# Second-layer weight sums from a load of their own, a sixth pair of split weights, and two output tiles weighted by VectorE

## The chip, the cores and the metric

The kernel runs on one core of one Trainium2 chip, as one launch. The metric is the time of an execution in device microseconds (us); lower is better. TensorE does the matrix products (the profile calls it PE, and its weight loads PEld), VectorE (DVE) and ScalarE (ACT) the work between them, GpSimd (POOL) issues the DMAs that add while they write and a few elementwise products, and SyncE (SP) issues the plain loads and stores. DMAs move data between HBM and the on-chip buffers.

## What is computed

One layer of a decoder trunk on 512 tokens of width 1024, in float32: a norm, one projection whose columns feed three groups of heads (dilated windows, gated linear attention, block-sparse attention), an output projection, a second norm, a feed-forward block of width 4096, and a final norm. The part that matters here is the end:

```python
x = x + mix @ w_out
h2 = rmsnorm(x, norm2_w)
x = x + jnp.square(jax.nn.relu(h2 @ w_ff1)) @ w_ff2
...
y = xf * lax.rsqrt(jnp.mean(xf * xf, axis=-1, keepdims=True) + EPS)
return (y * w.astype(jnp.float32)).astype(x.dtype)
```

## The kernel before

**Products in two halves.** Matrix products run on a reduced 32-bit type. Each operand is split into a high part `wh` (or `Ah`, `xh`, `yp`) that ScalarE makes by a copy, and a low part `wl` (`Al`) that VectorE makes by a subtraction; a product is then three matmuls: high by high, low by high, high by low. `parts` (line 282) splits a weight tile of 128 x 1024.

**The feed-forward block.** It has four chunks c of 1024 hidden columns, and each chunk two units: (1, c) makes `h` from the normed input and `w_ff1`, and (2, c) multiplies the squared `h` by `w_ff2` and adds to the residual `x3`. Each unit is a two-by-two block product done with seven products instead of eight (the Strassen-Winograd scheme). They run in the order of `PRODUCTS` (line 32), by number 0, 1, 3, 5, 2, 4, 6; the letters X, Y and Z name the accumulators, so the trace shows `f1X`, `f1Y`, `f1Z`, `f2X` and so on. Product 0 uses weight quadrant (0,0), product 1 uses (1,0), and the rest use sums of quadrants (with the signs put into the stored weights and the other operand). Every product comes in two halves, `ip` 0 and 1, with a weight tile of 512 KB each.

**Weight sums.** `fetch_ff` (line 316) loads the quadrants by SP in the order of `loads` (line 395). `sums_ff` (line 335) turns them into the sums: `plus` is a POOL DMA that adds a quadrant from HBM into a tile that is already there, `add` a VectorE addition. The main chain of a unit is one tile that becomes the operand of products 3, 2 and 6 in turn, by adding (0,1), then (1,1), then (1,0), each time only after the operand before has been split (`done(n)`: the event that `cut_ff`, line 406, fires). In the second-layer units that tile is the one of product 0 itself, so (0,1) is added only after product 0's split.

**The order of work.** `Plan` (class at line 101) writes the order of each engine's queue when the program is built. Streams of work (Python generators) are run against a clock with a cost for each operation; at each step it issues the operation that can start first, and by priority where several can. Costs are in `Op`: a DMA's size is divided by a rate, 280e3 bytes per us for a plain one and 170e3 for an adding one (line 78). `("wait", key)` and `("take", resource)` hold back a stream in the plan alone; on the chip, an operation starts when it is at the head of its engine's queue and the data and buffers that it touches are free. Tokens bound how far work runs ahead: `w` is the number of pairs of split weights (5, line 29: `WPAIRS`; the out-projection hands them back one by one in `let_go`, line 1072, and the last unit gets 3 more), `raw2` the raw weight tiles, `big` all large buffers (`BIGS`, 24, of 4 KB a partition). `SLOTS` (54, of 2 KB a partition) is the number of small buffers, which the plan doesn't model.

**The end.** `add` (line 1187) adds each product's accumulator to `x3`. When a half of a token tile t (0 to 3) is complete, `square_sum` (line 933) sums its squares. The half of a tile that is complete first is multiplied by the final norm's weights on POOL (`weighted`, line 1204, tile `xw`; `fw` is the weights); when the other half is complete, `final` (line 1211) makes the inverse root, weights and scales that other half on VectorE (tile `of`), scales `xw` on ScalarE, and stores both. For tiles 0 and 1 the first half is complete after product 1 of the last unit, for tiles 2 and 3 after product 4.

Of the kernel before, what the change touches and what calls it, by code (L numbers as in the profile page):

```python
# [13 lines left out]
OP = mybir.AluOpType  # L14
# [11 lines left out]
KO = (3, 4, 0, 1, 2, 5, 6, 7)  # L26
TAU = 1.0 / 16.0
LC, LT, LW, LN, WARM = 1.0, 0.5, 1.0, 0.0, 9
BIGS, SLOTS, WPAIRS = 24, 54, 5
NC = 4  # L30
LAG = 3
PRODUCTS = ((0, "X", True, ((0, 0),)), (1, "Y", True, ((0, 0),)), (3, "Z", True, ((1, 1),)), (5, "Z", False, ((0, 1),)),
# [3 lines left out]
class Op:  # L36


    def __init__(self, eng, method, args, kw):
        self.eng, self.method, self.args, self.kw = eng, method, args, kw  # L40
        self.out = args[0]
        outs = [args[0]]
        inner = [a for a in list(args[1:]) + [v for k, v in kw.items() if k != "accum_out"] if isinstance(a, bass.AP)]
        if kw.get("accum_out") is not None:
            outs.append(kw["accum_out"])
        if method == "tensor_tensor_reduce":
            outs.append(inner.pop())
        self.outs = [o.tensor.name for o in outs]
        self.ins = [a.tensor.name for a in inner] + (self.outs if "accum_op" in kw else [])
        n = 1  # L50
        for c in args[0].shape[1:]:
            n *= c
        if eng == "tensor":
            wide, long = inner[-1].dtype == F32, max(n, 250) / 2400
            if method != "matmul":
                self.cost = 0.109
            elif wide and inner[-1].shape[0] == 32:
                self.cost = 0.031
            elif wide:
                self.cost = 0.002 + max(n / 600 / (1 + (args[0].shape[0] == 64)), 0.21)  # L60
            elif inner[-1].shape[0] == 64:
                self.cost = max(n / 2260, 0.12) / 2
            else:
                self.cost = 0.0135 + long
        elif eng == "scalar":
            few = sum(a.shape[-1] == 1 and n > 4 for a in inner) + ("accum_out" in kw)
            self.cost = 0.09 + n / 1200 + 0.093 * few
        elif eng == "vector":
            many = method in ("tensor_scalar", "tensor_copy") and all(a.space == bass.MemoryType.SB for a in inner)
            rate = 0.52 if many else 6.25 if method == "reciprocal" else 1.04  # L70
            if method == "tensor_reduce":
                n = 512
            self.cost = 0.075 + n * rate / 1000
        elif eng == "gpsimd":
            self.cost = 0.15 + n * (0.9 if method == "memset" else 2.1) / 1000
        if method == "dma_start":
            self.cost = 0.9 if "accum_op" in kw else 0.06
            self.rate = 170e3 if "accum_op" in kw else 280e3
            self.size = 4 * n * args[0].shape[0]


# [16 lines left out]
PE, ACT, DVE, POOL, SP = (Engine(n) for n in ("tensor", "scalar", "vector", "gpsimd", "sync"))  # L98


class Plan:
# [17 lines left out]
    def fire(self, key, t=None):  # L119
        self.done[key] = self.now if t is None else t  # L120
# [78 lines left out]
def hybrid_block_kernel(ctx: ExitStack, tc: tile.TileContext, xT_d, x_d, w0_d, wv_d, wqk_d, wo_d, w1_d, w2_d,  # L199
# [9 lines left out]
    plan = Plan(nc, dict(BANKS, raw=3, w=WPAIRS, big=BIGS, raw2=3, part=5, lev=4, cnt=1))  # L209
    spawn, fire, give = plan.spawn, plan.fire, plan.give  # L210
    late = dict(copy=LC, tt=LT)

    def slot(name, dt=F32, shape=(128, 512)):
        return sp.tile(list(shape), dt, name=name, tag="slot", bufs=SLOTS)
# [4 lines left out]
    def small(name, shape):  # L219
        return sp.tile(list(shape), F32, name=name, tag="small_" + "_".join(map(str, shape)), bufs=16 if shape[1] <= 2 else 3)  # L220
# [110 lines left out]
    def give_raw():  # L331
        give("big")
        give("raw2")

    def sums_ff(u, ip):


        def plus(t, q):
            yield POOL.dma_start(t, quad_d(u, q, ip), accum_op=OP.add)

        def add(a, b):
            yield DVE.tensor_tensor(a, a, b, op=OP.add)

        def made(n, t):
            B[u, n, ip] = t
            fire(("B", u, n, ip))

        def done(n):
            yield ("wait", ("cut", u, n, ip))

        def loaded_(n):
            yield ("wait", ("quad", u, n, ip))
            return quads[u, n, ip]

        t = yield from loaded_(0)
        made(0, t)
        made(1, (yield from loaded_(1)))
        if u == units[0]:
            give_after(u, 0, ip)
            t = yield from loaded_(3)  # L360
            yield from plus(t, (0, 1))
            made(3, t)
            made(5, (yield from loaded_(5)))
            give_after(u, 5, ip)
            b12 = yield from loaded_(4)
            yield from plus(b12, (1, 1))
            made(4, b12)
            yield from done(3)
            yield from plus(t, (1, 1))
            made(2, t)  # L370
        else:
            b12 = None
            if u[0] == 1:
                b12 = yield from loaded_(4)
            b22 = yield from loaded_(5)
            made(5, b22)
            yield from done(0)
            yield from (add(t, b12) if b12 else plus(t, (0, 1)))
            made(3, t)
            yield from done(3)  # L380
            yield from plus(t, (1, 1))
            made(2, t)
            if b12:
                yield from add(b12, b22)
                made(4, b12)
                give_after(u, 5, ip)
            else:
                yield from done(5)
                yield from plus(b22, (0, 1))
                made(4, b22)  # L390
        yield from done(2)
        yield from plus(t, (1, 0))
        made(6, t)

    loads = {0: ((0, (0, 0)), (1, (1, 0)), (3, (0, 0)), (5, (1, 1)), (4, (0, 1))),
             1: ((0, (0, 0)), (1, (1, 0)), (4, (0, 1)), (5, (1, 1))),
             2: ((0, (0, 0)), (1, (1, 0)), (5, (1, 1)))}

    def give_after(u, n, ip):
        def stream():  # L400
            yield ("wait", ("cut", u, n, ip))
            give_raw()

        spawn(stream(), 0)
# [100 lines left out]
    st = {}  # L505
# [420 lines left out]
    x3 = {}  # L926
# [4 lines left out]
    ssq = {}  # L931

    def square_sum(t, half):

        q = small("ssq", (128, 1))
        yield ACT.activation(slot("junk"), x3[t, half], AF.Square, accum_out=q)
        if t in ssq:
            yield DVE.scalar_tensor_tensor(ssq[t], q, 1.0 / D, ssq[t], op0=OP.mult, op1=OP.add)
            fire(("ssq", t))
        else:  # L940
            ssq[t] = small("m", (128, 1))
            yield DVE.tensor_scalar(ssq[t], q, 1.0 / D, EPS, op0=OP.mult, op1=OP.add)

    def inv_rms(t):
        yield ("wait", ("ssq", t))
# [84 lines left out]
    def out_proj():  # L1030
# [41 lines left out]
        def let_go(i):  # L1072
            give("big")
            give("big")
            give("raw2")
            if i < WPAIRS:
                give("w")

        yield from take(2)
# [107 lines left out]
    def add(c, i, q, acc):  # L1187
        n, b_, _, targets = PRODUCTS[i]
        for blk, half in targets:
            t = 2 * blk + q  # L1190
            if c == NC - 1 and n != 6:
                yield ("prio", 1.3 + i)
            yield DVE.tensor_tensor(x3[t, half], x3[t, half], acc, op=OP.subtract if half and b_ == "X" else OP.add)
            if c == NC - 1 and not any((blk, half) in p[3] for p in PRODUCTS[i + 1:]):
                spawn(square_sum(t, half), -1 if n == 6 else 0)
                if t in ssq:
                    spawn(final(t, half), -1 if n == 6 else 0)
                else:
                    spawn(weighted(t, half), 9)
        if not any(p[1] == b_ for p in PRODUCTS[i + 1:]):  # L1200
            give(TAGS[2][b_][q])
        fire(("read", (2, c), b_, q))

    def weighted(t, half):
        yield ("wait", "fw")
        yield ("wait", ("w", ((2, NC - 1), 6, 1)))
        st["xw", t] = xw = slot("xw")
        yield POOL.tensor_tensor(xw, x3[t, half], fw[:, half * 512:half * 512 + 512], op=OP.mult)
        fire(("xw", t))

    def final(t, half):
        yield from inv_rms(t)
        y = st.pop(("inv", t))
        yield ("wait", ("xw", t))
        ts = slice(t * 128, (t + 1) * 128)
        a, b = (slice(h * 512, h * 512 + 512) for h in (half, 1 - half))
        of, xw = slot("of"), st.pop(("xw", t))
        yield DVE.scalar_tensor_tensor(of, x3[t, half], y, fw[:, a], op0=OP.mult, op1=OP.mult)
        yield SP.dma_start(out_d[ts, a], of)
        yield ACT.activation(xw, xw, AF.Copy, scale=y)  # L1220
        yield SP.dma_start(out_d[ts, b], xw)

    fw = None
# [202 lines left out]
```

## Time and profile before

| what | us |
|---|---|
| time, median of three runs | 590.65 (589.93 to 591.92) |
| the profiled execution's own time | 590.61 |
| its span, from the first to the last instruction | 588.8 |

The stages of that execution, with the busy time of the engines and the mean busy share of the DMA engines:

| stage | from to, us | PE | DVE | ACT | DMA share |
|---|---|---|---|---|---|
| first projection and gates | 0 to 34.8 | 31.5 | 23.3 | 22.1 | 0.84 |
| projections, attention, linear attention | 34.8 to 199.4 | 164.2 | 123.0 | 92.4 | 0.32 |
| output projection, second norm | 199.4 to 255.1 | 54.9 | 28.4 | 27.1 | 0.38 |
| unit (1, 0) | 255.1 to 298.0 | 41.9 | 36.5 | 34.7 | 0.74 |
| unit (2, 0) | 298.0 to 338.7 | 39.3 | 35.2 | 20.3 | 0.80 |
| units (1, 1) and (2, 1) | 338.7 to 417.2 | 78.4 | 66.1 | 49.6 | 0.74 |
| units (1, 2) and (2, 2) | 417.2 to 495.6 | 78.4 | 63.1 | 48.2 | 0.75 |
| unit (1, 3) | 495.6 to 535.9 | 40.3 | 27.0 | 26.7 | 0.62 |
| unit (2, 3) | 535.9 to 580.9 | 40.4 | 37.0 | 22.9 | 0.49 |
| after the last matmul | 580.9 to 588.8 | 0 | 2.6 | 2.5 | 0.35 |

A row such as `L129 DVE TENSOR_TENSOR h<-h,s x8: 684/687/3745` gives an engine, an operation, the tile written and the tiles read, the count, and the shortest, median and longest duration in ns. All operations are issued by one line (129) of the planner, so they are told apart by their tiles. `wraw` is a raw weight tile, `in_w` the weights in HBM. In an engine's queue in order of time, a row gives start, duration, operation, shapes and count; brackets give the idle time before it and what ended that. A share of a stretch in which the DMA engines are busy can read slightly over 1.

### The profile page before, as it was taken

How to read it: one execution, taken by the hardware profiler on the slowest of the kernel's cores; microseconds unless marked ns; L12 is line 12 of the kernel's file. 1: busy time of each engine (PE TensorE's matmuls, PEld its weight loads, DVE VectorE, ACT ScalarE, POOL GpSimd, SP SyncE). 2: the span in 40 equal slices, each digit the busy share in tenths (PEclk: the TensorE clock that was granted, in tenths of full speed). 3: DMA queues.
4: the chain of work that ended last, by engine and by line, in shares of the span. 5: the costliest groups of instructions: out<-in, count | busy, mean ns of one | idle time of the engine just before them, and what ended most of it. 6: DMA issues, size and time to landing. Idle time of an engine off the chain costs nothing.

```text
span 588.8 us, 9325 instructions
## 1 busy us (share of the span) xinstructions
PE 569.3 (97%) x3549; PEld 486.5 (83%) x3549; DVE 442.3 (75%) x788; ACT 346.4 (59%) x604; POOL 60.9 (10%) x81
## 2 busy tenths in 40 slices
PE   8999999999999999999999999999999999999794
PEld 7968888768876677899988699988999888998583
DVE  5789976754796724679789785799865998766994
ACT  6653426746585743667765356846377654676553
POOL 4020000000000000020012011120111110111301
PEclk9999999999999999999999999999999999999998
DMA  8921334041505630597687767778686694728802
GB/s 291 385 78 37 108 109 107 1 144 42 174 1 187 207 72 0 160 281 178 170 179 151 207 165 194 180 123 234 147 182 184 132 229 140 169 44 158 157 35 109
DMA packets 27069, 86.11 MB, mean 146 GB/s; under 512 B 3328, under 2 KB 3370, under 8 KB 27024
## 3 DMA queue, kind: packets, MB, share of 16 engines
q1 hardware_dynamic: 18864, 57.22, 28.7%
q0 software_dynamic: 8016, 28.28, 27.6%
q8 instruction: 28, 0.46, 0.3%
q14 instruction: 17, 0.14, 0.1%
q10 hardware_dynamic: 144, 0.01, 0.0%
HBM read 83.37 MB, written 2.13 MB: 145 GB/s over the span
## 4 chain that ended last, share of the span: by engine, by line
PE 65%; issue 13%; DVE 9%; DMA 9%; ACT 2%; POOL 0%; SPq 0%; POOLq 0%; ACTq 0%; DVEq 0%
PE qkps L129 11%; PE f1X L129 9%; DMA wraw<-in_w 8%; PE ops L129 7%; PE f2X L129 7%; PE vps L129 6%; PE f2Z L129 4%; PE f1Z L129 4%; DVE wl L129 3%; PE sps L129 2%; PE po L129 2%; PE ptp L129 2%; PE f1Y L129 2%; PE f2Y L129 2%; PE av L129 1%
## 5 line engine op out<-in xcount | busy, mean ns | idle before, releaser
L129 DVE TENSOR_TENSOR wl<-wraw,wh 128x1024 fp32r<-128x1024 f32 (+1 forms) x148 | 175.1, 1195 | 46.9 <-ACT wh L129 45.1
L129 ACT ACTIVATE wh<-wraw 128x1024 fp32r<-128x1024 f32 (+1 forms) x147 | 149.0, 1031 | 44.0 <-DMA wraw<-in_w 22.9
L129 POOL DMA_DIRECT2D wraw<-in_w x52 | 45.5, 880 | 470.7 <-DMA wraw<-in_w 219.7
L129 PE MATMUL f1X<-yp,wh 128*128 128x256 f32 x512 | 92.7, 283 | 0.0
L129 PEld LDWEIGHTS f1X<-yp,wh 128*128 128x128 f32 x512 | 80.1, 192 | 0.3
L129 PE MATMUL f1X<-yp,wl 128*128 128x256 f32 x256 | 72.7, 284 | 0.9 <-DVE wl L129 0.9
L129 PE MATMUL f2X<-wh,Ah 128*128 128x512 f32 x128 | 50.2, 392 | 0.9 <-DVE x L129 0.5
L129 PE MATMUL f2X<-wl,Ah 128*128 128x512 f32 x128 | 49.9, 390 | 0.5 <-DVE wl L129 0.5
L129 PEld LDWEIGHTS f1X<-yp,wl 128*128 128x128 f32 x256 | 49.1, 192 | 1.3 <-DVE wl L129 1.3
L129 PE MATMUL f2X<-wh,Al 128*128 128x512 f32 x128 | 49.9, 390 | 0.0
L129 ACT ACTIVATE h<-h 128x512 f32<-128x512 f32 x56 | 35.0, 627 | 22.6 <-DVE h L129 21.9
L129 PE MATMUL f1Z<-yp,wh 128*128 128x256 f32 x256 | 46.3, 283 | 0.0
L129 PE MATMUL qkps<-xh,wh 128*128 128x512 f32 x96 | 40.9, 426 | 0.0
L129 PEld LDWEIGHTS f1Z<-yp,wh 128*128 128x128 f32 x256 | 39.9, 192 | 0.0
L129 ACT ACTIVATE Ah<-h 128x512 fp32r<-128x512 f32 x40 | 24.1, 620 | 24.2 <-DVE h L129 24.2
L129 PE MATMUL qkps<-xh,wl 128*128 128x512 f32 x96 | 37.6, 392 | 0.0
L129 PE MATMUL qkps<-xl,wh 128*128 128x512 f32 x96 | 37.5, 391 | 0.0
L129 PE MATMUL f1Z<-yp,wl 128*128 128x256 f32 x128 | 36.2, 283 | 0.0
L129 ACT ACTIVATE P<-P,mn 128x512 f32<-128x512 f32 (+3 forms) x48 | 26.5, 554 | 15.6 <-DVE mn L129 15.5
L129 PEld LDWEIGHTS f2X<-wh,Ah 128*128 128x128 f32 x128 | 24.0, 188 | 6.9 <-DVE x L129 1.0
L129 DVE TENSOR_TENSOR Al<-h,Ah 128x512 fp32r<-128x512 f32 x40 | 27.0, 689 | 3.6 <-ACT Ah L129 3.5
L129 PE MATMUL f2Z<-wh,Al 128*128 128x512 f32 x64 | 25.6, 400 | 3.7 <-DVE Al L129 3.7
(225 smaller groups left out, 1199.8 us busy)
## 6 DMA issues: line engine op xcount, KB each, us to landing
wraw<-in_w SPq DMA_DIRECT2D x58, 512.0 KB, 4.8
wraw<-in_w POOLq DMA_DIRECT2D x52, 512.0 KB, 5.5
wraw<-in_wqk SPq DMA_DIRECT2D x12, 512.0 KB, 5.2
wraw<-in_wv SPq DMA_DIRECT2D x8, 512.0 KB, 5.2
wraw<-in_wo SPq DMA_DIRECT2D x8, 512.0 KB, 4.5
nb<-tab SPq DMA_DIRECT2D x12, 256.0 KB, 3.5
wraw<-in_w SPq DMA_DIRECT2D x8, 264.0 KB, 7.5
xT<-in_xT SPq DMA_DIRECT2D x8, 256.0 KB, 7.6
```

What stands on the lines that cost most here:

```text
L129: getattr(getattr(self.nc, op.eng), op.method)(*op.args, **op.kw)
```

## The change

Five things, in one diff:

- `BIGS` goes from 24 to 25, `SLOTS` from 54 to 52 (the same memory), and `let_go` hands back a sixth pair of split weights.
- The planner's rates of DMAs go from 280e3 to 380e3 bytes per us (plain) and from 170e3 to 190e3 (adding).
- In the second-layer units, quadrant (0,0) is loaded a second time, as number 3, between products 1 and 5; the sum for product 3 starts from that tile, with no wait for product 0's split, and product 0's tile is handed back after its split.
- `square_sum` orders the two halves of a tile by an event, `ssq0`.
- For tiles 0 and 1, `weighted` makes no product; `final` weights and scales both halves on VectorE and stores each.

```diff
-BIGS, SLOTS, WPAIRS = 24, 54, 5
+BIGS, SLOTS, WPAIRS = 25, 52, 5
...
-            self.rate = 170e3 if "accum_op" in kw else 280e3
+            self.rate = 190e3 if "accum_op" in kw else 380e3
...
             if u[0] == 1:
                 b12 = yield from loaded_(4)
-            b22 = yield from loaded_(5)
-            made(5, b22)
-            yield from done(0)
-            yield from (add(t, b12) if b12 else plus(t, (0, 1)))
+                b22 = yield from loaded_(5)
+                made(5, b22)
+                yield from done(0)
+                yield from add(t, b12)
+            else:
+                give_after(u, 0, ip)
+                t = yield from loaded_(3)
+                yield from plus(t, (0, 1))
+                b22 = yield from loaded_(5)
+                made(5, b22)
             made(3, t)
...
-             2: ((0, (0, 0)), (1, (1, 0)), (5, (1, 1)))}
+             2: ((0, (0, 0)), (1, (1, 0)), (3, (0, 0)), (5, (1, 1)))}
...
         q = small("ssq", (128, 1))
+        second = t in ssq
+        if not second:
+            ssq[t] = small("m", (128, 1))
         yield ACT.activation(slot("junk"), x3[t, half], AF.Square, accum_out=q)
-        if t in ssq:
+        if second:
+            yield ("wait", ("ssq0", t))
+            plan.done.pop(("ssq0", t))
             yield DVE.scalar_tensor_tensor(ssq[t], q, 1.0 / D, ssq[t], op0=OP.mult, op1=OP.add)
             fire(("ssq", t))
         else:
-            ssq[t] = small("m", (128, 1))
             yield DVE.tensor_scalar(ssq[t], q, 1.0 / D, EPS, op0=OP.mult, op1=OP.add)
+            fire(("ssq0", t))
...
-            if i < WPAIRS:
+            if i < WPAIRS + 1:
                 give("w")
...
     def weighted(t, half):
         yield ("wait", "fw")
+        if t < 2:
+            fire(("xw", t))
+            return
         yield ("wait", ("w", ((2, NC - 1), 6, 1)))
...
-        of, xw = slot("of"), st.pop(("xw", t))
-        yield DVE.scalar_tensor_tensor(of, x3[t, half], y, fw[:, a], op0=OP.mult, op1=OP.mult)
-        yield SP.dma_start(out_d[ts, a], of)
+        for h, s in ((half, a), (1 - half, b)) if t < 2 else ((half, a),):
+            of = slot("of")
+            yield DVE.scalar_tensor_tensor(of, x3[t, h], y, fw[:, s], op0=OP.mult, op1=OP.mult)
+            yield SP.dma_start(out_d[ts, s], of)
+        if t < 2:
+            return
+        xw = st.pop(("xw", t))
         yield ACT.activation(xw, xw, AF.Copy, scale=y)
         yield SP.dma_start(out_d[ts, b], xw)
```

## The prediction

> **What bounds the kernel now.** I read the page's busy table first, then TensorE's rows in the list of who waited for whom, then the chain and stretches of the second half, then the single instructions around the longest wait.
>
> ```profile
> PE 569.3 (97%) x3549; PEld 486.5 (83%) x3549; DVE 442.3 (75%) x788; ACT 346.4 (59%) x604; POOL 60.9 (10%) x81
> ```
>
> TensorE is busy for 97% of the span, so only its gaps, the start and the tail can be won. Its waits in the two feed-forward layers are few (total, times, longest):
>
> ```profile
> PE f2Z L129 <- DVE Al L129: 3.7, 1, 3.7
> ...
> PE f1X L129 <- DVE wl L129: 0.9, 2, 0.5
> PE f2Z L129 <- DVE x L129: 0.7, 1, 0.7
> PE f2X L129 <- DVE x L129: 0.5, 1, 0.5
> PE f2X L129 <- DVE wl L129: 0.5, 1, 0.5
> ```
>
> What a gap costs is read against the same products without one. The chain shows an undisturbed unit:
>
> ```profile
> 390.12 10.88 PE f2Z L129 x48
> 401.00 16.32 PE f2X L129 x72
> ```
>
> and the stretches show the same products elsewhere (start and end, length, busy time of PE, PEld, DVE, ACT, POOL, then clock, DMA share, GB/s):
>
> ```profile
> 319.80:338.74 18.94, 17.48 (x74) 13.20 (x72) 14.54 (x18) 7.71 (x9) 0.87 (x1) 1.00 0.75 206
> 338.74:417.16 78.42, 78.42 (x506) 71.86 (x504) 66.14 (x77) 49.60 (x66) 10.47 (x12) 1.00 0.74 175
> ...
> 546.80:564.26 17.46, 13.04 (x49) 9.88 (x48) 17.09 (x23) 8.32 (x14) 4.33 (x4) 0.90 0.61 109
> ```
>
> The two Z products (48 matmuls, 10.88 us) take 17.46 us in the last unit: **6.58 us lost**, with VectorE busy for 17.09 of it. The three late X products (72 matmuls, 16.32 us, so 0.2267 each and 5.44 a product) take 18.94 us in the first second-layer unit: **2.62 us lost**. The pair of units from 339 to 417 keeps TensorE busy for all 78.42 us: nothing to win there, only to lose. Now the last unit's gap. VectorE's queue, the tile `h` over the whole run, POOL, TensorE, then a stretch and the chain:
>
> ```profile
> 552.88 3.75 DVE L129 TENSOR_TENSOR h<-h,s 128x512 f32<-128x512 f32 x1
> 556.55 0.68 DVE L129 TENSOR_TENSOR Al<-h,Ah 128x512 fp32r<-128x512 f32 x1
> 557.15 1.21 DVE L129 TENSOR_TENSOR wl<-wraw,wh 128x1024 fp32r<-128x1024 f32 x1
> 558.29 0.68 DVE L129 TENSOR_TENSOR x<-x,f2Z 128x512 f32<-128x512 f32 x1
> 558.89 0.68 DVE L129 TENSOR_TENSOR Al<-h,Ah 128x512 fp32r<-128x512 f32 x1
> ```
>
> ```profile
> L129 DVE TENSOR_TENSOR h<-h,s x8: 684/687/3745, 305.6 to 552.9; 128x512 f32<-128x512 f32 x8
> ```
>
> ```profile
> 553.25 2.82 POOL L129 TENSOR_TENSOR xw<-x,fw 128x512 f32<-128x512 f32 x2
> ```
>
> ```profile
> 557.28 0.50 PE L129 MATMUL f2Z<-wh,Al 128*128 128x512 f32 x1 [3.69 <-DVE Al L129]
> ```
>
> ```profile
> 557.28:560.70 3.42, 3.42 (x9) 2.46 (x10) 3.42 (x6) 2.00 (x4) 0.00 (x0) 0.56 0.01 1
> ```
>
> ```profile
> 557.28 7.14 PE f2Z L129 x23
> ```
>
> Eight additions of this kind: median 687 ns, one of 3745. The long one lies over POOL's two `xw` products for tiles 0 and 1 (553.25 to 556.07) and lets the next instruction start 0.5 us after them. That `weighted` waits for the last weights is in the plan only: the product reads no weights, so on the chip it starts as soon as POOL's queue reaches it. The step from `h` to `Al` is 3.67 us where such a step is 0.60 (556.55 to 557.15): VectorE is held **3.07 us**. TensorE idles 3.69 us, and then the granted clock is 0.56 for 3.42 us. The 23 matmuls from 557.28 to the end of the Z products at 564.26 take 6.98 us instead of 23 x 0.2267 = 5.21: **1.77 us** more.
>
> **The change part by part**, against the profiled execution's 590.61 us (span 588.8, 1.8 around it; the median of the runs is 590.65, so the same).
>
> *Two outputs to VectorE.* POOL loses the two products of 553.25, ACT two scalings, VectorE gains two `of`. Rows: the tile `of`, VectorE's and POOL's queue in the last X products.
>
> ```profile
> L129 DVE SCALAR_TENSOR_TENSOR of<-x,y,fw x4: 750/750/752, 571.2 to 584.2; 128x512 f32<-128x512 f32 x4
> ```
>
> ```profile
> 573.42 1.28 DVE L129 SCALAR_TENSOR_TENSOR tmp<-tmp,m 128x1 f32<-128x1 f32 x1
> ...
> 575.66 0.68 DVE L129 TENSOR_TENSOR x<-x,f2X 128x512 f32<-128x512 f32 x1
> ```
>
> ```profile
> 573.39 1.29 POOL L129 TENSOR_TENSOR xw<-x,fw 128x512 f32<-128x512 f32 x1 [17.32 <-DVE tmp L129]
> ```
>
> Gain: 3.07 + 1.77 = 4.84 us, the clock's share because TensorE's short gaps elsewhere leave it at 1.00 (319.80 to 338.74 has three near 0.5 us). What is late next is VectorE's backlog. With its order unchanged, TensorE resumes near 557.28 - 3.07 = 554.2 and wants the second `Al` six matmuls on, at 555.6; that ends at 558.89 + 0.68 - 3.07 = 556.5. So 0.9 us can come back: the gain is 3.9 at least, 6.58 at most. The next part thins that backlog; I take **5.2**. The two added `of`, 1.5 us, stand on VectorE among the last additions `x`, which free a bank for TensorE. The one of 575.66 ends at 576.34; product 6's second half wants it at 564.26 + 2 x 5.44 + 2.72 = 577.9. These 1.5 us hide the `of`. Tile 2's `xw` stays on POOL, though, and beside it even a 128x1 operation took 1.28 us; if both meet, about 0.5 us shows. Cost 0, bounds 0 to 0.5. SP's queue issues the same number of output DMAs.
>
> The Trainium skill (SBUF — State Buffer, "Who interferes with whom") has a VectorE operation with two SBUF inputs and a GpSimd operation that reads SBUF lock each other out for a whole instruction. It adds that whoever issues first gets the port: `h` is recorded 0.37 us ahead of POOL, so by that rule `h` would have gone through, and its removal would win nothing. The recorded ends speak against it; the second rival prices that case from rows.
>
> *The first sum from its own load.* Before, quadrant (0,0) is split as product 0, and only then does POOL's DMA add (0,1) for product 3. The rows: POOL's queue, the chain through the first second-layer unit, VectorE's queue in the last unit, SP's queue, the page's DMA parts.
>
> ```profile
> 295.21 0.87 POOL L129 DMA_DIRECT2D wraw<-in_w  x1 [12.58 <-DVE wl L129]
> ```
>
> ```profile
> 295.21 11.55 DMA wraw<-in_w x2
> ...
> 321.91 9.77 DMA wraw<-in_w
> ```
>
> ```profile
> 539.58 1.23 DVE L129 TENSOR_TENSOR wl<-wraw,wh 128x1024 fp32r<-128x1024 f32 x1 [4.64 <-ACT wh L129]
> ```
>
> ```profile
> 259.52 7.25 SPq L129 DMA_DIRECT2D wraw<-in_w  x2
> ```
>
> ```profile
> wraw<-in_w SPq DMA_DIRECT2D x58, 512.0 KB, 4.8
> wraw<-in_w POOLq DMA_DIRECT2D x52, 512.0 KB, 5.5
> ```
>
> ```profile
> q1 hardware_dynamic: 18864, 57.22, 28.7%
> ```
>
> The additions leave at 295.21 and land at 306.76; the chain runs on through products 3, 2 and 6, and the last addition leaves at 321.91 and lands at 331.68. Product 6's second half starts at 319.80 + 2 x 5.44 + 1.36 = 332.0 if nothing is late, and the split before it takes about 2.2 us (1.21 on VectorE, an estimate of 1 on ACT), so it is 1.9 us late and TensorE loses its 2.62. Now the load for sum 3 takes the place in SP's queue of the two at 259.52 and 266.44 (product 5's today). With 4.8 to land and 5.5 to add it is there before 280; POOL idles then (12.58 before 295.21). Product 3's splits wait for buffers alone, and the later links move up by an estimated 4 us, twice what is missing. Gain 0 to 2.62; I take **2.3**. In the last unit the same takes away VectorE's idle 4.64 us before 539.58, into which splits can move from the backlog above: hence 5.2 and not 3.9.
>
> The price is eight more plain loads, 4.19 MB. At 57.22 MB in 28.7% of 588.8 us that is 12.4 us of DMA time, 3.1 in a pair of units: a share of 0.78 instead of 0.74 in 78.42 us. The lead of the loads over their splits hides it; without that cover a split is late by a load, 4.8 us. I take 0. Product 5's quadrant is loaded two places later and still well ahead. POOL's queue gets no more additions; one that stands at its head before its load has landed holds the others, again for at most a load.
>
> *A sixth pair of split weights, 25 large and 52 small buffers.* No instruction is added. Splits can run half a product further ahead; two fewer small buffers can add a wait where one is reused. 0, bounds -1.2 (the first unit's two waits for `wl`, 0.9, and an estimated 0.3 of restarting) and +1. *The planner's rates* (380 and 190 GB/s) change no work, but the order of every queue is written anew: 0, bounds as in the third rival. *The tail* keeps its operations: 0.
>
> Sum: 590.61 - 5.2 - 2.3 = **583.1 us**.
>
> **Rivals.** (1) *Only the lock goes.* The new order doesn't use the earlier sums, VectorE's backlog stays, the first unit waits as before: 590.61 - 3.9 = 586.7. For it: VectorE is busy 17.09 of 17.46 us. Against: its 4.64 idle us lie just ahead. (2) *The lock isn't the cause*; `h` was slow from something else, such as the DMA traffic: 590.61 - 2.3 = 588.3. Against: seven like it, in units whose DMA share is higher (0.74 against 0.61), were ordinary, and the next `xw` has a slow neighbour too. (3) *Slower: splits planned too early.* At 380 and 190 GB/s the planner believes additions done sooner than the chip does them (5.5 median, 9.77 in the first unit); ACT takes its queue in order, so a split placed ahead of its data holds the activations behind it. Waits of ACT for a weight DMA (total, times, longest):
>
> ```profile
> ACT wh L129 <- DMA wraw<-in_w: 22.9, 11, 4.6
> ```
>
> The price is 2.62 us for a late link, as today's. If four links of the first two units' chains are late, 590.61 - 4.84 + 4 x 2.62 = 596.3; it decides from two on, where 5.24 eats the 4.84, and from three on it is over 0.3% slower (593.6). Against: eleven such waits stand in the order of today, and TensorE loses 2.62 and about 1.2 us by them.
>
> **How the numbers follow.** 583.1 and its neighbours (580.2 to 585.2): 0.58. Rival 1 (585.2 to 588.0): 0.24. Rival 2: 0.06. Rival 3: 0.08. Below 580.2: 0.04. The lower end is everything won (6.58 + 2.62 + 1.2 from 590.61); the upper end is rival 1 with 1.3 us of new waits. Together they hold 0.82. Faster by over 0.3% (0.3% is about what a measurement of this kernel can tell from no change; below 588.9): 0.58 + 0.04 + 0.24 and a part of rival 2, less a little for losses not thought of: 0.87. Within 0.3%: 0.06. Slower: 0.07.
>
> **What would show it.** Right: no `h` addition above 0.7 us, clock 1.00 through the last unit, its Z products near 12.3 us; the first unit's late X products near 16.6; 66 plain loads instead of 58; POOL's first `xw` only among the last X products. Wrong: a long `h` still there; ACT waiting for a weight DMA in 255 to 340 with TensorE behind it; a gap in a middle unit; TensorE waiting for an `x` behind an `of`.

## The result, and the profile after

The changed kernel takes **588.58 us** (median of 15 runs, 584.09 to 597.19) against 590.84 of the kernel before on the same chip. The ratios compare fast runs alone and leave out four of these fifteen (592.93 to 597.19; the median of the other eleven is 587.57): **0.9942, interval 0.9914 to 0.9970**. The direction was forecast, the size was not: 583.1 was put down, and 588.58 lies outside 580.2 to 588.0. A second set gave 590.81 against 591.25, ratio 0.9978 (0.9944 to 1.0011). By the intervals the gain is 1.8 to 5.1 us in the first set and -0.7 to 3.3 us in the second, where 7.5 had been expected.

The profiled execution took 590.57 us with a span of 588.8, to the digit the span of before. The list of who waited for whom, TensorE's rows in the feed-forward layers, has a single row left (total, times, longest):

```profile
PE f1X L129 <- DVE h L129: 6.5, 2, 3.9
```

All the waits shown of before are gone, and this one is new. The groups of instructions by tile show that POOL's products no longer hold an `h`: none is long, and the first product is at 573.7. (Beside it an `of` of VectorE takes 1777 ns where its median is 750, but TensorE waits for none.)

```profile
L129 DVE TENSOR_TENSOR h<-h,s x8: 680/681/686, 305.2 to 552.4; 128x512 f32<-128x512 f32 x8
```

```profile
L129 POOL TENSOR_TENSOR xw<-x,fw x2: 1294/1508/1721, 573.7 to 576.7; 128x512 f32<-128x512 f32 x2
```

The stretches say where the time went instead. First the three places that lost time before, then two middle units (columns as in the prediction: from and to, length, PE, PEld, DVE, ACT, POOL, clock, DMA share, GB/s):

```profile
317.68:334.00 16.32, 16.32 (x73) 13.51 (x72) 16.32 (x20) 7.94 (x9) 0.00 (x0) 1.00 0.58 165
...
553.34:564.22 10.88, 10.88 (x49) 9.01 (x48) 10.88 (x18) 8.19 (x13) 0.87 (x1) 1.00 0.60 99
...
254.69:295.90 41.21, 41.21 (x346) 41.20 (x344) 35.28 (x53) 34.05 (x60) 6.19 (x7) 1.00 0.89 234
...
334.00:378.68 44.68, 42.06 (x338) 41.85 (x337) 26.14 (x29) 27.98 (x38) 5.32 (x6) 0.96 0.75 199
416.78:463.68 46.90, 42.97 (x337) 42.76 (x336) 25.91 (x28) 27.91 (x38) 5.29 (x6) 0.93 0.69 181
```

The late X products of the first second-layer unit take the undisturbed 16.32 us, the last unit's Z products the undisturbed 10.88 at full clock. The units (1, 1) and (1, 2), which took 40.31 before, take 44.68 and 46.90. The same reading for every unit and for the kernels that follow (length of each unit, from its first matmul to the next unit's first, in TensorE's queue of the profiled execution):

| us | first matmul | (1,0) | (2,0) | (1,1) | (2,1) | (1,2) | (2,2) | (1,3) | (2,3) |
|---|---|---|---|---|---|---|---|---|---|
| before | 255.13 | 42.88 | 40.73 | 40.31 | 38.11 | 40.31 | 38.11 | 40.31 | 44.86 |
| changed | 254.69 | 41.21 | 38.10 | **44.68** | 38.10 | **46.90** | 38.11 | 40.65 | 38.27 |
| changed, second set | 254.78 | 41.20 | 38.10 | **44.54** | 38.10 | **43.55** | 38.11 | 41.18 | 38.27 |
| only the outputs | 254.18 | 42.86 | 41.51 | 40.31 | 38.11 | 40.31 | 38.11 | 40.31 | 41.18 |
| outputs and rates | 253.43 | 43.10 | 38.11 | 40.31 | 38.11 | 40.31 | 38.11 | 40.31 | 39.92 |
| outputs and own load | 256.29 | 42.87 | 38.91 | **43.67** | 38.51 | **41.65** | 38.11 | **41.84** | 38.37 |
| changed, without own load | 253.92 | 42.21 | 40.19 | 40.32 | 38.10 | 40.32 | 38.10 | 40.32 | 38.31 |
| changed, addition held back | 253.48 | 42.03 | 38.69 | 40.31 | 38.11 | 40.31 | 38.11 | 40.31 | 38.27 |

Between the first two rows 1.67 + 2.63 + 6.59 = 10.89 us are won in the first two units and the last, and 4.37 + 6.59 + 0.34 = 11.30 lost in three (1, c) units. The layer also starts 0.44 us earlier, so the two profiled executions end together.

**How the new gap comes about.** In unit (1, 1), the queues in order of time (start, duration, operation; in brackets the idle time before it and what ended that):

```profile
346.48 3.58 POOL L129 DMA_DIRECT2D wraw<-in_w  x4 [8.41 <-DMA wraw<-in_w]
```

```profile
362.61 2.00 ACT L129 ACTIVATE wh<-wraw 128x1024 fp32r<-128x1024 f32 x2 [4.77 <-DMA wraw<-in_w]
362.68 0.28 PE L129 MATMUL f1X<-yp,wl 128*128 128x256 f32 x1
363.70 1.22 DVE L129 TENSOR_TENSOR wl<-wraw,wh 128x1024 fp32r<-128x1024 f32 x1 [5.71 <-ACT wh L129]
364.84 0.68 DVE L129 TENSOR_TENSOR h<-h,f1X 128x512 f32<-128x512 f32 x1
...
365.57 0.38 PE L129 MATMUL f1X<-yp,wh 128*128 128x256 f32 x1 [2.62 <-DVE h L129]
```

Read it from the end. TensorE has done product 2 of the late X products (357.04 + 48 x 0.12 = 362.8) and wants the accumulator that VectorE's `h` addition empties. That addition needs nothing late; it stands in VectorE's queue behind a `wl`, which waits 5.71 us for ScalarE's `wh`, which waits 4.77 us for a weight tile. The tile is the sum for product 6, needed on TensorE only one product later. Its addition is the last of the four that POOL issues from 346.48 on. The same four in the view by tile (duration min/median/max and starts; who waited; issue to landing):

```profile
L129 POOL DMA_DIRECT2D wraw<-in_w x4: 875/1360/1504, 346.5 to 348.6; - x4
...
  ACT wh L129: 4.8, 1
...
DMA to landing us min/median/max: 5.3/8.7/14.0
```

The one issued at 348.55 lands 14.0 us later, at 362.6; the median of all 52 went from 5.5 to 6.2 us only. The trace's rows don't name the quadrants; the order in which each program puts its additions on POOL's queue tells which four they are ("early" is the second layer's (0,1) for product 3, which the own load has made possible; 6a and 6b are the first layer's last additions, for the two halves of product 6):

```
unit (1,1), changed kernel:            early a, 6a, early b, 6b
unit (1,1), early addition held back:  6a, 6b, early a, early b
unit (1,2), changed kernel:            early a, early b, 6a, 6b
```

In unit (1, 2) both early ones are ahead; the first stands at the head of POOL's queue for 10.02 us until its load lands:

```profile
430.64 0.88 POOL L129 DMA_DIRECT2D wraw<-in_w  x1 [10.02 <-DMA wraw<-in_w]
431.85 2.67 POOL L129 DMA_DIRECT2D wraw<-in_w  x3 [0.34 <-issue]
```

The last of these lands after 13.8 us, TensorE waits 3.93 us. The clock makes both gaps dearer. Stretches after the gap of (1, 1) and after the one of (1, 2), columns as above:

```profile
365.57:366.40 0.83, 0.82 (x7) 0.83 (x8) 0.83 (x1) 0.83 (x2) 0.00 (x0) 1.00 0.42 94
366.40:369.80 3.40, 3.40 (x19) 3.40 (x18) 1.99 (x3) 3.37 (x6) 0.00 (x0) 0.50 0.86 312
369.80:373.00 3.20, 3.20 (x28) 3.20 (x28) 2.24 (x4) 2.11 (x4) 0.00 (x0) 1.00 0.36 136
...
449.66:455.17 5.51, 5.51 (x26) 5.51 (x27) 2.82 (x3) 4.27 (x7) 0.00 (x0) 0.50 0.82 277
```

After 2.62 us of idle, half clock for 3.40 us: 1.7 us more, and 2.62 + 1.7 is the 4.37 lost. After 3.93 us, half clock for 5.51 us: about 2.7 more, and 3.93 + 2.7 is the 6.59 lost. The length of the gap hangs on when single DMAs land, and half clock doesn't follow every such gap (experiment 9). The changed kernel's times spread over 13 us, those of its versions without these gaps (experiments 2 and 3, four runs each) over 0.4 and 0.7.

### The profile page after: what moved, and what is told of

Read it like the earlier page. It is cut to its first block, busy times and chain, and to the rows that moved or that the text cites. A ratio compares the mean times of both kernels' runs of the same rounds, so it can differ in the third digit from the quotient of the medians.

```text
span 588.8 us, 9350 instructions
## 1 busy us (share of the span) xinstructions
PE 570.7 (97%) x3549; PEld 490.1 (83%) x3549; DVE 439.6 (75%) x792; ACT 345.7 (59%) x600; POOL 58.8 (10%) x79
## 3 DMA queue, kind: packets, MB, share of 16 engines
q0 software_dynamic: 8016, 28.28, 26.3%
## 5 line engine op out<-in xcount | busy, mean ns | idle before, releaser
L129 ACT ACTIVATE wh<-wraw 128x1024 fp32r<-128x1024 f32 (+1 forms) x147 | 150.3, 1034 | 59.6 <-DMA wraw<-in_w 23.4
L129 PE MATMUL f1X<-yp,wh 128*128 128x256 f32 x512 | 96.8, 291 | 6.6 <-DVE h L129 6.5
L129 PEld LDWEIGHTS f1X<-yp,wh 128*128 128x128 f32 x512 | 83.3, 199 | 7.5 <-DVE h L129 7.2
L129 PE MATMUL f1X<-yp,wl 128*128 128x256 f32 x256 | 74.1, 290 | 0.0
L129 PEld LDWEIGHTS f1X<-yp,wl 128*128 128x128 f32 x256 | 50.9, 199 | 0.0
L129 DVE CUSTOM_DVE_ANT_0 P<-sps,nb 128x512 f32<-128x512 f32 (+3 forms) x48 | 21.7, 483 | 9.7 <-PE sps L129 9.6
L129 PEld LDWEIGHTS f2X<-wl,Ah 128*128 128x128 f32 x128 | 24.0, 188 | 5.0
```

The source lines that it names most:

```text
L129: getattr(getattr(self.nc, op.eng), op.method)(*op.args, **op.kw)
```

## The experiments

The theories. The **queue** theory: early additions in POOL's queue delay the additions for the first layer's product 6, and the split planned for these holds VectorE's queue. The **rates** theory (the third rival): the planner's rates put splits too early, with or without the own load. The **traffic** theory: the eight added loads take DMA time from the others. All ratios are against the kernel before on the same chip, with their 95% intervals.

**1. Only the outputs and `ssq0`**, on the kernel before (three of the five parts left out).

```diff
-BIGS, SLOTS, WPAIRS = 25, 52, 5
+BIGS, SLOTS, WPAIRS = 24, 54, 5
...
-            self.rate = 190e3 if "accum_op" in kw else 380e3
+            self.rate = 170e3 if "accum_op" in kw else 280e3
...
-             2: ((0, (0, 0)), (1, (1, 0)), (3, (0, 0)), (5, (1, 1)))}
+             2: ((0, (0, 0)), (1, (1, 0)), (5, (1, 1)))}
...
-            if i < WPAIRS + 1:
+            if i < WPAIRS:
```

> The kernel before with the change's last part alone (both halves of tiles 0 and 1 weighted by VectorE, and the event ssq0). Lock theory: the 3.7 us addition h is 0.7 us, the last unit's Z products take 12 to 13.5 us instead of 17.46 at a clock of 1.00, the first unit's 2.6 us and the X products' 1.2 us stay: 4 to 5 us less than before, 586 to 587. If the products on POOL were not the cause: a long h still there, time as before. No gap in the middle units by any theory but the one that blames the square sums.

588.02 us, ratio 0.9935 (0.9917 to 0.9953), span 585.0. The group of `h` and TensorE's waits:

```profile
L129 DVE TENSOR_TENSOR h<-h,s x8: 681/685/693, 304.6 to 552.7; 128x512 f32<-128x512 f32 x8
```

```profile
PE f2Z L129 <- DVE Al L129: 1.3, 2, 0.7
PE f2X L129 <- DVE x L129: 1.1, 2, 0.5
```

The long `h` goes with POOL's two products beside it, so these held it. The last unit wins 44.86 - 41.18 = 3.68 us and still waits for VectorE's backlog.

**2. The changed kernel without the own load**: sums and loads of the second layer as before.

```diff
-             2: ((0, (0, 0)), (1, (1, 0)), (3, (0, 0)), (5, (1, 1)))}
+             2: ((0, (0, 0)), (1, (1, 0)), (5, (1, 1)))}
...
-                b22 = yield from loaded_(5)
-                made(5, b22)
-                yield from done(0)
-                yield from add(t, b12)
-            else:
-                give_after(u, 0, ip)
-                t = yield from loaded_(3)
-                yield from plus(t, (0, 1))
-                b22 = yield from loaded_(5)
-                made(5, b22)
+            b22 = yield from loaded_(5)
+            made(5, b22)
+            yield from done(0)
+            yield from (add(t, b12) if b12 else plus(t, (0, 1)))
```

> The changed kernel with the second layer's sums as before (no load of their own, product 3 waits for product 0's split); rates, sixth pair, buffers and outputs as changed. Queue theory (the early additions for the second layer's product 3 stand in POOL's queue among those for the first layer's product 6 and delay them): no gap in units (1,1) and (1,2), 78.4 us a pair; the first unit's loss of up to 2.6 us comes back at least in part; 583 to 587. If the rates, the sixth pair or the smaller pool of buffers make the gaps: they stay (4 and 6 us), 588 to 594.

581.78 us, 0.9835 (0.9816 to 0.9854): better than expected, and 6.8 us faster than the changed kernel. The gaps of the middle units are gone, at the new rates: the rates alone don't make them.

**3. The changed kernel with the early addition held back.** One line; all loads stay, and only the plan's order changes.

```diff
                 t = yield from loaded_(3)
+                yield ("wait", ("B", (1, u[1]), 6, ip))
                 yield from plus(t, (0, 1))
```

> The changed kernel, but the addition (0,1) for the second layer's product 3 waits, in the plan, until the addition for product 6 of the first-layer unit ahead of it has been issued: same loads, same additions, another order in POOL's queue. Queue theory: no gap in the middle units and nothing lost in the first and last: about 10.4 us less than before, 580 to 582. Rates, pairs or buffers: gaps of 4 to 6 us stay, 586 to 592.

**579.78 us, 0.9801 (0.9781 to 0.9820)**: faster than both kernels. POOL's queue in unit (1, 1), the landing of the addition issued at 348.75, the two units, and the DMA issues:

```profile
347.01 0.87 POOL L129 DMA_DIRECT2D wraw<-in_w  x1 [8.94 <-DVE wl L129]
348.75 2.67 POOL L129 DMA_DIRECT2D wraw<-in_w  x3 [0.86 <-DVE wl L129]
```

```profile
L129 POOL DMA_DIRECT2D wraw<-in_w x1: 875/875/875, 348.7 to 348.7; - x1
...
DMA to landing us min/median/max: 6.0/6.0/6.0
```

```profile
334.20:374.51 40.31, 40.31 (x337) 40.30 (x336) 26.12 (x28) 27.94 (x38) 5.29 (x6) 1.00 0.80 216
412.62:452.93 40.31, 40.31 (x337) 40.30 (x336) 26.09 (x28) 27.93 (x38) 5.29 (x6) 1.00 0.78 210
```

```profile
wraw<-in_w SPq DMA_DIRECT2D x66, 512.0 KB, 4.7
```

This is the experiment that shows the order to be a cause: in unit (1, 1), and in (1, 2), VectorE's 27 operations and SP's 10 loads follow in the same order in both traces. Addition 6b leaves at 348.75, no earlier than in the changed kernel (348.55); as second of the four it lands in 6.0 us, as last in 14.0. The slow one is now an early addition (12.6 us), for which nobody waits. The 66 loads are there, and the DMA share of the unit is higher (0.80 against 0.75): against the traffic theory.

**4. The changed kernel at the old rates.**

```diff
-            self.rate = 190e3 if "accum_op" in kw else 380e3
+            self.rate = 170e3 if "accum_op" in kw else 280e3
```

> The changed kernel with the planner's old rates (280e3 and 170e3). Queue theory: the early additions still stand among those for product 6 in units (1,1) to (1,3), so gaps of a few us stay in the middle units: 584 to 591. If the optimistic rates place splits too early: the gaps go, 580 to 582.

583.54 us, 0.9861 (0.9838 to 0.9884). Early additions and product 6's alternate in POOL's queue here too, yet no gap opens in the late X products; unit (1, 0) takes 44.11 us, and (1, 1) 42.16 because TensorE waits 1.6 us for an `h` of ScalarE. In unit (1, 2) the order on POOL's queue is early a, 6a, early b, 6b, as in the changed kernel's (1, 1), and 6b lands late as well, 11.1 us after its issue at 432.00. VectorE's queue is what differs:

```profile
440.22 1.23 DVE L129 TENSOR_TENSOR wl<-wraw,wh 128x1024 fp32r<-128x1024 f32 x1 [3.09 <-ACT wh L129]
443.57 0.69 DVE L129 TENSOR_TENSOR h<-h,f1X 128x512 f32<-128x512 f32 x1 [2.12 <-PE f1X L129]
445.90 1.23 DVE L129 TENSOR_TENSOR wl<-wraw,wh 128x1024 fp32r<-128x1024 f32 x1 [1.64 <-ACT wh L129]
```

The two `wl` are the splits of product 6's two halves. At the old rates the second stands behind the first `h`; in the changed kernel, which differs by the rates alone, both stand ahead of it (363.70 before 364.84 above). A miss for the queue theory as it was put: the changed kernel's gap takes both, a late addition and a split that the plan puts ahead of an `h`. The order on POOL's queue makes the first, the new rates the second, so the rates theory is half right.

**5. Held back, with the old outputs**: POOL weights all four tiles again.

```diff
-        if t < 2:
-            fire(("xw", t))
-            return
         yield ("wait", ("w", ((2, NC - 1), 6, 1)))
...
-        for h, s in ((half, a), (1 - half, b)) if t < 2 else ((half, a),):
-            of = slot("of")
-            yield DVE.scalar_tensor_tensor(of, x3[t, h], y, fw[:, s], op0=OP.mult, op1=OP.mult)
-            yield SP.dma_start(out_d[ts, s], of)
-        if t < 2:
-            return
-        xw = st.pop(("xw", t))
+        of, xw = slot("of"), st.pop(("xw", t))
+        yield DVE.scalar_tensor_tensor(of, x3[t, half], y, fw[:, a], op0=OP.mult, op1=OP.mult)
+        yield SP.dma_start(out_d[ts, a], of)
```

> The kernel of the held addition (579.8 us) with the outputs of tiles 0 and 1 as before: POOL multiplies their first halves. Lock theory: the two products on POOL hold a VectorE operation of the last unit for about 3 us again, wherever the new order places them; if that operation is one that TensorE waits for, 583 to 585, with a clock under 1.00 behind the gap. If the lock only mattered because VectorE had no slack there: the long operation shows but the time stays within 1 us of 579.8.

580.73 us, 0.9816 (0.9797 to 0.9835): 0.95 us more than experiment 3 by the medians, with intervals that overlap. The group of `h` that was held before stays ordinary (681/686/689 ns). POOL's two products now lie over the next group, and one of these is held:

```profile
545.40 3.47 POOL L129 TENSOR_TENSOR xw<-x,fw 128x512 f32<-128x512 f32 x2
```

```profile
L129 DVE TENSOR_TENSOR h<-h x2: 679/1226/1773, 547.6 to 549.3; 128x512 f32<-128x512 f32 x2
```

So the long operation shows and the time stays within 1 us: the products still hold VectorE, but TensorE loses little by it (the last unit takes 38.62 us instead of 38.27). In this order the outputs are worth about 1 us by the medians, instead of the 3.5 of experiment 1.

**6. Experiment 1 with the sixth pair and 25 and 52 buffers.**

```diff
-BIGS, SLOTS, WPAIRS = 24, 54, 5
+BIGS, SLOTS, WPAIRS = 25, 52, 5
...
-            if i < WPAIRS:
+            if i < WPAIRS + 1:
```

> The kernel before with the new outputs (588.0 us alone) and the sixth pair with its buffers; old rates, no load of its own. If the sixth pair is what freed VectorE's backlog in the last unit (2.9 us still lost there with the outputs alone) and the first unit's late sums (3.4 us): 582 to 584. If the rates did it: 587 to 588.

588.27 us, 0.9951 (0.9929 to 0.9972), as experiment 1. Underneath is a trade: the last unit takes 38.30 instead of 41.18, but in (2, 0) TensorE waits 3.1 us for a `wh` and the unit takes 44.38 instead of 41.51.

**7. Experiment 1 with the new rates.**

```diff
-            self.rate = 170e3 if "accum_op" in kw else 280e3
+            self.rate = 190e3 if "accum_op" in kw else 380e3
```

> The kernel before with the new outputs and the new rates; five pairs, no load of its own. If the rates (a new order of all queues) freed the backlog and the first unit: 582 to 584. If the sixth pair did: 587 to 588.

581.98 us, 0.9851 (0.9829 to 0.9872): 6.0 us less than experiment 1 by the medians (about 5 by the ratios), from two constants that are no work on the chip. The first and the last addition of unit (2, 0) in POOL's queue, first in experiment 1, then here:

```profile
294.24 0.87 POOL L129 DMA_DIRECT2D wraw<-in_w  x1 [12.56 <-DVE wl L129]
...
321.05 0.88 POOL L129 DMA_DIRECT2D wraw<-in_w  x1 [2.30 <-DVE wl L129]
```

```profile
287.93 0.88 POOL L129 DMA_DIRECT2D wraw<-in_w  x1 [12.47 <-DVE wl L129]
...
317.01 0.88 POOL L129 DMA_DIRECT2D wraw<-in_w  x1 [3.00 <-DVE wl L129]
```

The first addition waits for a `wl` in both, the split of product 0; here that comes earlier, so the chain moves up by 6.3 us at its head and 4.0 at its end, without an own load, and the unit takes 38.11 us.

**8. Experiment 1 with the own load**, old rates, five pairs.

```diff
-             2: ((0, (0, 0)), (1, (1, 0)), (5, (1, 1)))}
+             2: ((0, (0, 0)), (1, (1, 0)), (3, (0, 0)), (5, (1, 1)))}
...
-            b22 = yield from loaded_(5)
-            made(5, b22)
-            yield from done(0)
-            yield from (add(t, b12) if b12 else plus(t, (0, 1)))
+                b22 = yield from loaded_(5)
+                made(5, b22)
+                yield from done(0)
+                yield from add(t, b12)
+            else:
+                give_after(u, 0, ip)
+                t = yield from loaded_(3)
+                yield from plus(t, (0, 1))
+                b22 = yield from loaded_(5)
+                made(5, b22)
```

> The kernel before with the new outputs and the second-layer sums from a load of their own; old rates, five pairs. By the prediction's reason (the earlier sum frees the first unit and the last unit's backlog): 2.9 and up to 3.4 us less than the outputs alone, 582 to 583. By the queue theory, gaps come where the early additions stand among those for product 6 in the middle units, so 585 to 592 with gaps in (1,1) to (1,3).

590.80 us, 0.9993 (0.9979 to 1.0006): 2.8 us slower than experiment 1. The own load does what it was credited with (unit (2, 0) from 41.51 to 38.91, the last from 41.18 to 38.37) and gives it back in the (1, c) units and in a start 2.1 us later. POOL's order in unit (1, 1) is 6a, early a, early b, 6b; its four additions and who waited:

```profile
L129 POOL DMA_DIRECT2D wraw<-in_w x4: 875/960/1194, 354.8 to 359.0; - x4
...
  ACT wh L129: 4.1, 2
...
DMA to landing us min/median/max: 6.5/10.9/13.9
```

So a split waits for a late addition at the old rates too; TensorE waits 2.4 us there, for product 6's own `wh`.

**9. The changed kernel once more**, for the spread. No edit.

> The changed kernel once more, for the scatter of its times (584 to 597 in fifteen executions, where the held addition gave 579.5 to 580.2 in four). Queue theory: the gaps lie at the same places, in the late X products of units (1,1) and (1,2), and only their length differs, with the landing of the last of four additions; half clock behind those that are long. If the scatter came from the chip and not from this order, the gaps would lie elsewhere or the time would be the profiled one within 1 us.

590.81 us (584.22 to 595.35), 0.9978 (0.9944 to 1.0011). The gaps are at the same places (table above); in unit (1, 1) the landing times agree:

```profile
DMA to landing us min/median/max: 5.4/8.6/14.0
```

In (1, 2) the first early addition leaves at 428.26 instead of 430.64, the gap is 2.97 us instead of 3.93 and the unit takes 43.55 instead of 46.90. Most of that difference isn't the gap but the clock, which stays whole behind it:

```profile
448.65:455.00 6.35, 6.35 (x53) 6.35 (x54) 5.29 (x7) 6.32 (x11) 0.00 (x0) 1.00 0.72 248
```

In (1, 1) of the same execution the clock reads 0.50 behind a gap of 2.60 us (from 365.64). Half clock behind the long gaps had been expected; it came behind the shorter of the two.

**10. Held back until product 6 has been split**, not only until its addition has been issued.

```diff
-                yield ("wait", ("B", (1, u[1]), 6, ip))
+                yield ("wait", ("cut", (1, u[1]), 6, 1))
```

> The changed kernel with the early addition held in the plan until product 6 of the first-layer unit is split (in e3 only until its addition is issued), so that the four additions are no longer in flight together. If only the order within POOL's queue counts: 579.8 as e3, within 1 us. If sharing of the DMA engines by additions in flight counts as well: up to 1.5 us less than e3.

580.47 us, 0.9816 (0.9785 to 0.9847), within the intervals of experiment 3. The wait is in the plan alone, and on the chip POOL's queue issues what stands next. In unit (1, 1) the four leave as close together as in experiment 3:

```profile
347.98 0.87 POOL L129 DMA_DIRECT2D wraw<-in_w  x1 [8.85 <-DVE wl L129]
349.72 2.67 POOL L129 DMA_DIRECT2D wraw<-in_w  x3 [0.86 <-DVE wl L129]
```

So this run repeats the order of experiment 3 with the same result; what four additions in flight cost each other it doesn't test.

**11. Only the rates**, on the kernel before (the edit of experiment 7).

> The kernel before with the new rates alone. The new order left VectorE slack in the last unit (e7 loses 1.6 us there, 582.0 in all). Lock theory with slack: POOL's two products cost 0 to 1.5 us more than in e7, 582 to 583.5. If the outputs are worth their 3.5 us in any order: 585.5.

583.43 us, 0.9878 (0.9849 to 0.9907). The group of `h` that was held before is ordinary (687/689/695 ns), but POOL's two products, one of 2382 ns, lie over the next group and hold two of its additions:

```profile
551.02 4.08 POOL L129 TENSOR_TENSOR xw<-x,fw 128x512 f32<-128x512 f32 x2
```

```profile
L129 DVE TENSOR_TENSOR h<-h x8: 687/689/1783, 315.3 to 553.9; 128x512 f32<-128x512 f32 x8
```

The last unit takes 40.89 us against 39.92 with the new outputs. By the medians these are worth 1.45 us here, with intervals that overlap.

**12. Experiment 3 with five pairs.**

```diff
-            if i < WPAIRS + 1:
+            if i < WPAIRS:
```

> The kernel of the held addition with five pairs of split weights. If the sixth pair does nothing once the rates are new (e2 with it 581.8, e7 without it and without the load 582.0): 579.5 to 580.5. If it is needed for the sums' lead to reach TensorE: 581 to 584.

579.94 us, 0.9822 (0.9790 to 0.9854): in this kernel the sixth pair does nothing that can be measured.

## Why the prediction was wrong

**Right: the lock.** POOL's products held VectorE, TensorE idled behind it, the clock halved. "3.9 at least" without the backlog's thinning was the estimate; experiment 1, which has the outputs alone, wins a little less in that unit, 3.68 us. In experiments 5 and 11 POOL's two products hold the `h` that they meet there, to 1773 and 1783 ns. The rule of the Trainium skill weighed there (SBUF — State Buffer, "Who interferes with whom": whoever issues first gets the port) would have had nothing won. Experiment 1 agrees with its lock, and by the recorded starts not with that order.

**Right in sum, wrongly credited: 5.2 and 2.3.** The changed kernel wins 6.59 in the last unit, and 2.63 in the first second-layer unit, plus 1.67 in (1, 0) that I had costed at 0 with -1.2 as the bound. I put the 2.3, and the 1.3 between 3.9 and 5.2, down to the own load. It can do that (experiment 8), but the rates do it without the load (experiment 7), and little is left for it then: with both, and the early addition kept out of the way, 579.78 stand against 581.78 without the load, 2.0 us for eight loads.

**Wrong: "POOL's queue gets no more additions; one that stands at its head before its load has landed holds the others, again for at most a load", and with it the extra loads at 0.** This is the step that failed. The count is right: 52 before and after. But I counted the additions and not their places. An addition that no longer waits for product 0's split can leave half a unit earlier, and there it meets the first layer's last additions. The wait at the head is no more than a part of it (10.02 us at 430.64; in unit (1, 1) the addition that matters isn't issued late at all). Four additions that leave within 2.1 us share the DMA engines, and the last lands after 14.0 us where two in that unit had landed after 5.3 and 7.8 before. Counted from the unit's first matmul, 6b lands at 28.6 us in the changed kernel, at 27.0 before and at 20.6 with the early addition held back; before, its split stood behind the first `h` in VectorE's queue, as in experiment 4. I had priced a late split by a plain load, 4.8. That the time ends close to the upper end of the range is luck: 10.89 us won and 11.30 lost stand in none of its sums.

**Wrong: "nothing to win there, only to lose", and no term for the loss.** The prediction read the middle units as free of gaps and took their order as given, at "0, bounds as in the third rival". The third rival's mechanism is what happened, "a split placed ahead of its data holds the activations behind it", and half of it by its own way: the new rates put both splits of product 6 ahead of the first `h` (experiment 4). The other half it did not have: the data is late by POOL's order, in the (1, c) units, with VectorE's `h` as what is held. Two such places were enough, as written ("it decides from two on"), but they cost 4.37 and 6.59 us instead of 2.62 each: gaps of 2.62 and 3.93 us, and half clock behind both. A gap in a middle unit was named as a sign of being wrong, and it came. With the own load as its cause the rival deserved far more than the 0.08 that it got.

**Wrong in size: the planner's rates.** They were priced at 0 or a loss. Experiments 1 and 7 show 6.0 us won by the medians, the largest single part of the change; 11 shows 7.8 against the kernel before.

In one sum, by medians (the kernel before had 590.84 to 591.54 in these sets): outputs from 591.54 to 588.02; rates to 581.98; sixth pair and buffers to 581.78, nothing; the own load up to 588.58 or, held back, down to 579.78.

Open: what makes half clock follow one gap and not another; how much the additions in flight delay each other by themselves; why the layer's start moves between 253.4 and 256.3 from plan to plan; and `SLOTS`, which wasn't tried by itself.

## What to carry to other kernels

When an operand is made available earlier, look at what its next step will be queued among: here a DMA that adds was harmless where it was late and cost two gaps where it overtook one that is needed sooner, though neither the number of additions nor their bytes changed. In an in-order queue the wait that the profile names (`DVE h`) need not be the late thing; follow the rows back until one ends on a DMA, then look at its place among its neighbours. And take constants of a planner as edits with a price of their own: change them alone before you credit a redesign with what they gave.

## What was unexpected about the hardware

The fourth of four additions of 512 KB issued within 2.1 to 2.3 us landed after 14.0, 13.8 and 14.0 us in three places, the quickest of the four after 5.3 or 5.4. The page of the changed kernel gives the cost:

```profile
q1 hardware_dynamic: 20016, 61.42, 30.3%
q0 software_dynamic: 8016, 28.28, 26.3%
```

By these rows 512 KB take 26.3% x 588.8 us x 0.524 / 28.28 = 2.87 us of all 16 engines as an addition (q0) and 1.52 as a plain load. That is an estimate from the whole run; four additions and the three plain loads issued in the same 16 us come to 16.0, and from the first issue to the last landing it was 16.1. The DMA view of these 16.1 us comes near it: the engines are busy for 69.6% with q0 and 23.4% with q1.

A TensorE gap of 2.62 us was followed, after 0.83 us at full speed, by 3.40 us at clock 0.50. Half clock also followed one of 2.60 us (second set) and one of 3.11 us (experiment 6, unit (2, 0)), but behind 2.38 us (experiment 8, unit (1, 1)) and 2.97 us (second set, unit (1, 2)) the clock read 1.00. The Trainium skill (TensorE: Matmul & The Clock Gate, "Why this matters for your kernels") advises against idle gaps above about 3 us; the trace shows that one a little shorter can already pay, and that the length alone doesn't decide. After a gap of 1.54 us, in unit (2, 0) of experiment 2, the clock read 1.00.
